# Attention with bias on one core: first loads in float32 in order of need, a first group of three pairs, single banks on VectorE, a ring of 56 banks

## The chip, the cores and the metric

The kernel runs on one core of one Trainium2 chip. The core has TensorE (PE, matrix products into PSUM), VectorE (DVE), ScalarE (ACT), GpSimd (POOL) and SyncE (SP), each with its own in-order queue, and 16 DMA engines that serve the queues of SP, ACT and POOL. The metric is the device time of one execution in microseconds (us); less is better. Before the change the median of three runs is 277.88 us (274.79 to 279.21).

## What is computed

Four batches of eight heads, 1024 positions, head size 64, all float32 in and out:

```python
scores = scale * np.matmul(q, k.transpose(0, 1, 3, 2))      # scale = 1/8
scores = scores + bias                                       # one bias of 1024 x 1024 for all heads
scores_max = np.max(scores, axis=-1, keepdims=True)
attn = np.exp(scores - scores_max) / (np.sum(np.exp(scores - scores_max), axis=-1, keepdims=True) + 1e-8)
return np.matmul(attn, v).astype(np.float32)
```

## The kernel before

**Tiling.** The 32 heads are 16 *pairs*. Rows of q, k, v, bias and the output are dealt out so that partition p holds rows 8p to 8p+7; *chunk* c (0 to 7) is row 8p+c of every p, and "bias row c" below is the slice of bias for chunk c of the queries (128 x 1024 float32, 0.52 MB). The query chunks are handled in three *phases*: A is chunks 6 and 7, B is 3 to 5, C is 0 to 2. The pairs go in three *groups*: pairs 0 and 1 (phases A, B, C), 2 to 7 (C, B, A), 8 to 15 (A, B, C). Within a phase the pairs of the group follow one another, and within a pair its two heads. One head in one phase is two *steps*, one into each of the PSUM buffers sx and sy (three banks of 128 x 512 float32 each): 192 steps in all, 0 to 191. A step of phase A fills two banks, one of B or C three; 512 banks in all.

**A step.** PE computes scores transposed, keys on partitions (`s_fill`, L182). At the first step of a phase, if the phase before was another one, bias is put into PSUM by matmuls with an identity (L169). After that PSUM is never cleared: each fill adds the new head's product and takes the old head's away, with 128 contraction rows of which 64 are the new head and 64 the negated old one. This is why there are two copies of the transposed k and q: KA and QA hold the two heads of a pair (one of q negated), KB and QB hold the first head of the pair beside the second head of the pair before. ACT then takes exp of the buffer and writes bfloat16 into the ring E (`s_exp`, L195), 44 banks long (`EB`). PE multiplies blocks of E with V into `po` (`av_blocks`, L257; V has a column of ones, which gives the row sums), and VectorE divides and stores (`evac`, L267 to L269). No maximum is taken off.

**VectorE's share of exp.** For some pairs of steps the last bank of each is not done by ACT but by VectorE: it is brought into fixed point (`d_fixed`, L207), and six operations (`d_steps`, L219 to L224) on both banks together, 1024 columns, make exp by a polynomial. The result stands in `e` tiles (three buffers) and not in E. 40 of 512 banks go this way.

**Operands.** Each pair's k, q and v are loaded by POOL's queue with a cast to bfloat16 on the way (`load_qk`, `load_v`; three buffers for k and q each, two for v). PE transposes k and q (L137, into `px`), VectorE moves them from PSUM to KA (`k_out`, L140) and QA (`q_out`, L147), makes the negated q (`qn`, L151), and four DMAs on SP's queue copy the halves into KB and QB (L142, L144, L152, L154). KA to QB and V hold nine pairs (`RP`).

**The start** is written by hand (L273 to L324, without the planner): five float32 loads on SP and ACT (k and chunks 6 and 7 of q of pair 0, bias rows 6 and 7) with casts on VectorE and ACT; everything else casting on POOL's queue, in the order k 1, q 1, rest of q 0, v 0, bias rows 3 to 5, v 1, bias rows 0 to 2, k 2, q 2. Seven dummy matmuls keep PE busy until the first data.

**The order of the rest** is made by a planner in the kernel's own Python (`pe_fill`, `pe_piece`, `pe_av`, `pe_pick`, `act_pick`, `dve_pick`) at build time. It keeps a clock for each engine, gives each operation an assumed cost, and at each turn emits the one that can start first; each engine's queue is then fixed. Its numbers are assumptions: `raw_at`, `v_at`, `bias_at` are landing times of the first loads, `DMAL` (2600 ns) is the time from issue to landing of a copy into KB or QB, 1350 ns is the spacing of loads, `RING` (12 steps) says when products with V are overdue, `URG` (6 steps) when a transpose is urgent, `DLIM` how much work VectorE may have queued before it takes banks.

Of the kernel before, what the change touches and what calls it, by code (L numbers as in the profile page):

```python
# [16 lines left out]
def kernel(  # L17
# [11 lines left out]
    nc = tc.nc  # L29
# [14 lines left out]
    EB = 44  # L44
# [6 lines left out]
    de = ctx.enter_context(tc.tile_pool(name="de", bufs=3))  # L51
# [15 lines left out]
    scr = consts.tile([P, 4608], F32)  # L67
    ys = [scr[:, 1024 * i:1024 * (i + 1)] for i in range(2)]
    sf, sb, sp = scr[:, 2048:3072], scr[:, 3072:4096], scr[:, 4096:4608].bitcast(I16)
    c6f, c7f, k0f = scr[:, :1024], scr[:, 1024:2048], scr[:, 2048:3072]  # L70
    q0f = scr[:, 3072:3328]
# [5 lines left out]
    groups = [(range(0, 2), "ABC"), (range(2, 8), "CBA"), (range(8, NP), "ABC")]  # L77
# [61 lines left out]
    def k_out(pr, px):  # L139
        nc.vector.tensor_copy(KA[:, pr % RP, :], px.rearrange("p c q -> p (c q)"))  # L140
        if pr > 1:
            nc.sync.dma_start(out=KB[:D, pr % RP, :], in_=KA[:D, pr % RP, :])  # L142
        if pr + 1 < NP:
            nc.sync.dma_start(out=KB[D:, (pr + 1) % RP, :], in_=KA[D:, pr % RP, :])  # L144

    def q_out(pr, px):
        nc.vector.tensor_scalar(QA[:, pr % RP, :], px.rearrange("p c q -> p (c q)"), sgn[:, :1], None, op0=ALU.mult)  # L147

    def q_neg(pr, c0=0):
        qn = qnp.tile([P, NCH * P], BF, name="qn")  # L150
        nc.vector.tensor_scalar(qn[:], QA[:, pr % RP, :], -1.0, None, op0=ALU.mult)  # L151
        nc.sync.dma_start(out=QB[:D, pr % RP, c0:], in_=qn[:D, c0:])  # L152
        if pr + 1 < NP:
            nc.sync.dma_start(out=QB[D:, (pr + 1) % RP, :], in_=qn[D:, :])  # L154

# [49 lines left out]
    def d_fixed(ch, j, s, b):  # L205
        y = ys[ch % 2].bitcast(I32)
        i = nc.vector.tensor_scalar(y[:, j * 512:(j + 1) * 512], XY[s % 2][:, b * 512:(b + 1) * 512],  # L207
                                    scale * LOG2E * 65536.0, 127.0 * 65536.0, op0=ALU.mult, op1=ALU.add)
        read_of(s, i)

    def d_steps(ch):
        y = ys[ch % 2]
        e = de.tile([P, 1024], BF, name="e")
        dtiles[ch] = e
        lo = y.bitcast(U16).rearrange("p (q w) -> p q w", w=2)[:, :, 0]
        hi = y.bitcast(I16).rearrange("p (q w) -> p q w", w=2)[:, :, 1]
        v_ = nc.vector
        return [
            (690, lambda: v_.tensor_scalar(sf, lo, G / 65536.0, None, op0=ALU.mult)),  # L219
            (690, lambda: v_.tensor_scalar(sp, hi, 0.0, 128.0, op0=ALU.max, op1=ALU.mult)),  # L220
            (1217, lambda: v_.scalar_tensor_tensor(y, sf, U1, sf, op0=ALU.add, op1=ALU.mult)),  # L221
            (1217, lambda: v_.scalar_tensor_tensor(sb, sf, U2, sf, op0=ALU.add, op1=ALU.mult)),  # L222
            (1217, lambda: v_.scalar_tensor_tensor(sb, sb, V2, sp.bitcast(BF), op0=ALU.add, op1=ALU.mult)),  # L223
            (1217, lambda: v_.scalar_tensor_tensor(e[:], y, V1, sb, op0=ALU.add, op1=ALU.mult)),  # L224
        ]
# [11 lines left out]
    def e_block(s, col):  # L237
        b = col // 512
        if (s, b) in d_of:
            ch, j = d_of[s, b]  # L240
            return dtiles[ch][:, j * 512 + col % 512:j * 512 + col % 512 + P]
        return E[:, e_pos[s] * 512 + col:e_pos[s] * 512 + col + P]
# [28 lines left out]
    with tc.manual_schedule():  # L271

        nc.sync.dma_start(out=k0f[:, :NCH * D], in_=kf[0][:, 0])  # L273
        nc.scalar.dma_start(out=c6f, in_=bf_[:, 6, :])
        nc.sync.dma_start(out=q0f.rearrange("p (t x) -> p t x", t=2), in_=qf[0][:, :, 6 * D:])
        nc.sync.dma_start(out=k0f[:, NCH * D:], in_=kf[0][:, 1])
        nc.scalar.dma_start(out=c7f, in_=bf_[:, 7, :])
# [6 lines left out]
        kr0 = raw.tile([P, 2, NCH, D], BF, name="kr")  # L284
        qr0 = raw.tile([P, 2, NCH, D], BF, name="qr")
        load_qk(1)
        nc.gpsimd.dma_start(out=qr0[:, :, :6, :].rearrange("p t c d -> p t (c d)"), in_=qf[0][:, :, :6 * D])
        load_v(0)
        nc.gpsimd.dma_start(out=btraw[:, 3:6, :], in_=bf_[:, 3:6, :])
        load_v(1)  # L290
        nc.gpsimd.dma_start(out=btraw[:, :3, :], in_=bf_[:, :3, :])
        load_qk(2)
        nc.vector.tensor_scalar(ident8[:], ident[:], 1.0 / scale, None, op0=ALU.mult)
# [5 lines left out]
        for i in range(7):  # L299
            dummy(4)  # L300
        nc.vector.tensor_copy(qr0[:, :, 6:, :], q0f.rearrange("p (t c d) -> p t c d", t=2, c=2))
        nc.scalar.copy(kr0[:, 0, :, :], k0f[:, :NCH * D].rearrange("p (c d) -> p c d", d=D))
        pq = ps.tile([P, 2, P], BF, tag="xa", name="px")
        transpose_pe(pq, qr0, 6, 2)
        pk = ps.tile([P, NCH, P], BF, tag="xb", name="px")
        for c in range(NCH):
            nc.tensor.transpose(pk[:D, c, :], kr0[:, 0, c, :], ident[:])
        nc.vector.tensor_scalar(QA[:, 0, 6 * P:], pq.rearrange("p c q -> p (c q)"), sgn[:, :1], None, op0=ALU.mult)
        nc.scalar.copy(QB[:D, 0, 6 * P:], pq[:D].rearrange("p c q -> p (c q)"))
        nc.vector.tensor_copy(btraw[:, 6, :], c6f)  # L310
        nc.scalar.copy(KA[:D, 0, :4 * P], pk[:D, :4].rearrange("p c q -> p (c q)"))
        nc.vector.tensor_copy(KA[:D, 0, 4 * P:], pk[:D, 4:].rearrange("p c q -> p (c q)"))
        s_fill(0)
        s_exp(0, 2, 0)
        nc.vector.tensor_copy(kr0[:, 1, :, :], k0f[:, NCH * D:].rearrange("p (c d) -> p c d", d=D))
        for c in range(NCH):
            nc.tensor.transpose(pk[D:, c, :], kr0[:, 1, c, :], ident[:])
        nc.vector.tensor_copy(btraw[:, 7, :], c7f)
        nc.vector.tensor_copy(KA[D:, 0, :], pk[D:].rearrange("p c q -> p (c q)"))
        s_fill(1)  # L320
        nc.vector.tensor_scalar(QB[D:, 1, 6 * P:], QA[D:, 0, 6 * P:], -1.0, None, op0=ALU.mult)
        nc.vector.tensor_copy(KB[D:, 1, :], KA[D:, 0, :])
        nc.vector.memset(VV[:, :, :, D:], 1.0)
        s_exp(1, 2, 2)  # L324
# [3 lines left out]
        T0 = 8500.0  # L328
        t_act, t_pe, t_dve = T0 + 1830, T0 + 1100, T0 + 1500
        fill_end = [T0, T0 + 900]  # L330
        act_end = [T0 + 915, T0 + 1830]
        fix_end = {}
        x_free = {"xa": T0, "xb": T0 + 1000}
        bias_at = {"A": T0, "B": 15400, "C": 20600}
        raw_at = {(0, 0): 10800, (1, 1): 8500, (1, 0): 9800, (2, 1): 22000, (2, 0): 23300}
        v_at = {0: 11200, 1: 16700}
        dma_t = 23500.0
        kA = {0: T0}
        qA = {(0, "A"): T0}
        kB, qB = {}, {(0, "A"): T0}  # L340
        kB[1] = (T0 + 1900,)
        qB[1, "A"] = (T0 + 1500,)
        pieces = [(1, 1, 0, 4), (1, 1, 4, 4), (1, 0, 0, 4), (1, 0, 4, 4), (0, 0, 0, 6)]
        for pr in range(2, NP):
            pieces += [(pr, w, 0, NCH) for w in (1, 0)]
        cur, cur_tag = [], [None]
        v_ready = {}
        v_todo = [0, 1]
        next_load = 3
        next_v = 2  # L350
        dve_q = []
        mark = {}
        open_ch = {}
        nch = 0
        av_u = 0
        av_items = {}
        av_tag = {}
        av_left = {}
        e_at = {}
        d_at = {}  # L360
        d_load = 0.0
        ch_wait = []
        e_live = [(0, 0, 2), (1, 2, 2)]

        def banks_act(s):
            pa = steps[s // 2][0]
            nb = nbanks(pa)
            return nb - 1 if s in mark else nb
# [8 lines left out]
        def av_make(u):  # L377
            pa, pr, i0 = units[u]
            items = []
            for s in range(2 * i0, 2 * i0 + 4):  # L380
                for b in range(nbanks(pa)):
                    items.append((s, b))
            av_items[u] = items
            for s in range(2 * i0, 2 * i0 + 4):
                av_left[s] = banks_act(s)

        for u in range(NU):
            av_make(u)
# [9 lines left out]
        def operands(s):  # L398
            pa, pr, h, restart = steps[s // 2]
            pk_ = "A" if pa == "A" else "F"  # L400
            if restart:
                if pr not in kA or (pr, pk_) not in qB and (pr, "F") not in qB:
                    return None
                t = qB.get((pr, pk_), qB.get((pr, "F")))
                return max(kA[pr], max(t) if isinstance(t, tuple) else t, bias_at[pa])
            if h:
                t = qA.get((pr, pk_), qA.get((pr, "F")))
                if pr not in kA or t is None:
                    return None
                return max(kA[pr], t)  # L410
            t = qB.get((pr, pk_), qB.get((pr, "F")))
            if pr not in kB or t is None or len(kB[pr]) < 2 or len(t) < 2:
                return None
            return max(max(kB[pr]), max(t))

        def pe_fill():
# [8 lines left out]
            def emit(t):  # L425
                nonlocal nch, d_load
                pa, pr, h, restart = steps[s // 2]
                if h == 0 and s % 2 == 0:
# [356 lines left out]
```

## Time and profile before

| what | value |
|---|---|
| median of three runs | 277.88 us (274.79 to 279.21) |
| the profiled execution: its own time / its span | 276.14 us / 274.0 us |
| mean granted TensorE clock in it | 0.956 |
| busy: PE / DVE / ACT / POOL | 235.8 / 212.9 / 223.9 / 35.5 us |
| exp on ACT (L195) | 96 of three banks, 88 of two, 8 of one |
| L257 products with V, 128 x 65 | 2048, 88.2 us |
| VectorE's exp chain (L207, L219 to L224) | 20 of two banks, 152.5 us |
| loads with a cast (POOL's queue) | 13.83 MB as bfloat16 |
| copies into KB / QB, issue to landing | median 4.6 / 5.1 us, longest 7.3 / 7.4 |

The profile is of one execution; durations are of single instructions, and instructions of one engine overlap by a little, so that their sum is above the engine's busy time. A line of the page's groups reads: source line, engine, operation, result and operand, shapes and count; busy us and mean ns of one; idle time before, and what ended it.

### The profile page before, as it was taken

Reading aid. Unit: us, or ns where it says so; the run is one execution under the profiler, and the core shown is the slowest. Engines: PE = TensorE matmul, PEld = TensorE weight load, DVE = VectorE, ACT = ScalarE, POOL = GpSimd, SP = SyncE. Lnnn points to the kernel's source line nnn. Section 1 sums busy time; section 2 is a strip of 40 time slices with the busy share of each in tenths; the row PEclk is TensorE's granted clock in tenths of the full one; section 3 lists DMA queues with packets and bytes.
Section 4 is the critical chain, followed back from the end, with each engine's and each line's share of the span. In section 5 each row is a group of like instructions: output and inputs, shape, how many; then the busy total and the mean of one; then the engine's idle time right before and its main releaser. Section 6 shows DMA issues by size and latency. Waiting matters only on the chain.

```text
span 274.0 us, 9158 instructions
## 1 busy us (share of the span) xinstructions
PE 235.8 (86%) x3999; PEld 194.7 (71%) x3999; DVE 212.9 (78%) x337; ACT 223.9 (82%) x197; POOL 35.5 (13%) x55
## 2 busy tenths in 40 slices
PE   4889998876899999899895985689998989899983
PEld 1777875654687887699794864577886767778673
DVE  0566988864798999899898586527899998998962
ACT  3277999874798999989997664547999999999993
POOL 8151235233300102100242000000000000000000
PEclk9599999997999999999999799759999999999999
DMA  7999999999961245812999762000221110111112
GB/s 235 221 208 231 206 182 208 211 248 230 178 159 31 44 124 135 156 45 85 139 198 196 159 136 60 19 22 19 60 71 31 60 31 29 32 60 31 60 37 80
DMA packets 31575, 31.94 MB, mean 117 GB/s; under 512 B 2544, under 2 KB 27184, under 8 KB 31536
## 3 DMA queue, kind: packets, MB, share of 16 engines
q0 software_dynamic: 13072, 13.83, 33.1%
q1 hardware_dynamic: 18176, 16.49, 20.5%
q10 hardware_dynamic: 288, 1.05, 1.1%
q8 instruction: 31, 0.51, 0.8%
q14 instruction: 8, 0.07, 0.1%
HBM read 29.36 MB, written 8.39 MB: 138 GB/s over the span
## 4 chain that ended last, share of the span: by engine, by line
PE 44%; ACT 27%; DMA 10%; issue 9%; DVE 7%; POOL 1%; ACTq 1%; SPq 0%; POOLq 0%; DVEq 0%
ACT E L195 27%; PE po L257 13%; PE sx L182 12%; PE sy L182 11%; DMA QB<-qn 5%; PE px L137 3%; DMA scr<-in_q_dram 2%; PE sx L169 2%; DMA vs<-in_v_dram 2%; PE sy L169 2%; DMA KB<-KA 1%; DVE scr L207 1%; DVE ob L268 1%; DVE e L224 1%; DVE KA L140 1%
## 5 line engine op out<-in xcount | busy, mean ns | idle before, releaser
L195 ACT ACTIVATE E<-sx 128x1024 bf16<-128x1024 f32 (+2 forms) x96 | 118.0, 1229 | 23.3 <-PE sx L182 18.7
L195 ACT ACTIVATE E<-sy 128x1024 bf16<-128x1024 f32 (+2 forms) x96 | 117.9, 1228 | 16.1 <-PE po L257 9.3
L257 PE MATMUL po<-VV,E 128*128 128x65 bf16 x1888 | 79.1, 195 | 0.4 <-ACT E L195 0.4
L257 PEld LDWEIGHTS <-E 128*128 128x128 bf16 x1888 | 73.1, 99 | 5.3 <-ACT E L195 0.5
L182 PEld LDWEIGHTS <-KA 128*128 128x128 bf16 (+1 forms) x732 | 55.5, 100 | 23.5 <-issue 11.0
L182 PEld LDWEIGHTS <-KB 128*128 128x128 bf16 x548 | 42.4, 100 | 28.0 <-issue 18.8
L182 PE MATMUL sx<-QB,KB 128*128 128x128 bf16 (+2 forms) x274 | 31.7, 257 | 11.6 <-ACT E L195 4.4
L182 PE MATMUL sy<-QA,KA 128*128 128x128 bf16 (+1 forms) x320 | 36.8, 255 | 5.2 <-ACT E L195 3.9
L182 PE MATMUL sx<-QA,KA 128*128 128x128 bf16 (+1 forms) x320 | 37.1, 257 | 3.7 <-ACT E L195 2.9
L182 PE MATMUL sy<-QB,KB 128*128 128x128 bf16 (+2 forms) x274 | 31.7, 256 | 6.0 <-ACT E L195 5.8
L268 DVE TENSOR_TENSOR ob<-po,rs 128x384 f32<-128x384 f32 (+1 forms) x48 | 24.6, 513 | 1.6
L267 DVE RECIPROCAL rs<-po 128x6 f32<-128x6 f32 (+1 forms) x48 | 9.0, 188 | 20.2 <-PE po L257 20.2
L221 DVE SCALAR_TENSOR_TENSOR scr<-scr 128x1024 f32<-128x1024 f32 x20 | 24.4, 1221 | 0.3
L223 DVE SCALAR_TENSOR_TENSOR scr<-scr 128x1024 f32<-128x1024 f32 x20 | 24.4, 1220 | 0.3
L224 DVE SCALAR_TENSOR_TENSOR e<-scr 128x1024 bf16<-128x1024 f32 x20 | 24.4, 1219 | 0.2
L222 DVE SCALAR_TENSOR_TENSOR scr<-scr 128x1024 f32<-128x1024 f32 x20 | 24.3, 1216 | 0.0
L207 DVE TENSOR_SCALAR scr<-sx 128x512 int32<-128x512 f32 x20 | 13.8, 688 | 9.0 <-PE sx L182 8.8
L128 POOL DMA_DIRECT2D vs<-in_v_dram x16 | 11.5, 716 | 55.7 <-DVE VV L132 44.0
L207 DVE TENSOR_SCALAR scr<-sy 128x512 int32<-128x512 f32 x20 | 13.8, 689 | 4.6 <-ACT E L195 2.5
L122 POOL DMA_DIRECT2D kr<-in_k_dram x15 | 10.9, 727 | 30.2 <-PE px L137 30.1
L169 PEld LDWEIGHTS <-btraw 128*128 128x128 bf16 x152 | 11.8, 151 | 3.6 <-issue 3.1
L140 DVE COPY KA<-px 128x1024 bf16<-128x1024 bf16 x15 | 10.3, 685 | 5.2 <-PE px L137 5.2
(57 smaller groups left out, 162.5 us busy)
## 6 DMA issues: line engine op xcount, KB each, us to landing
out_dram<-ob SPq DMA_DIRECT2D x32, 192.0 KB, 2.0
vs<-in_v_dram POOLq DMA_DIRECT2D x16, 256.0 KB, 5.6
kr<-in_k_dram POOLq DMA_DIRECT2D x15, 256.0 KB, 7.4
qr<-in_q_dram POOLq DMA_DIRECT2D x15, 256.0 KB, 7.4
KB<-KA SPq DMA_DIRECT2D x28, 128.0 KB, 4.6
QB<-qn SPq DMA_DIRECT2D x28, 128.0 KB, 5.1
out_dram<-ob SPq DMA_DIRECT2D x16, 128.0 KB, 2.3
btraw<-in_bias_dram POOLq DMA_DIRECT2D x2, 768.0 KB, 14.1
```

The lines of the kernel that those rows point to most:

```text
L128: nc.gpsimd.dma_start(out=vs.rearrange("p (t c) d -> p t (c d)", t=2), in_=vf[pr])
L140: nc.vector.tensor_copy(KA[:, pr % RP, :], px.rearrange("p c q -> p (c q)"))
L169: nc.tensor.matmul(ps_[:, cc:cc + P], btraw[:, c + j, :].rearrange("p (kp kc) -> p kc kp", kc=NCH)[:, kc, :], ident8[:], start=cc // 512 n ...
L182: nc.tensor.matmul(o, lhsT, rhs, start=False, stop=True, skip_group_check=True)
L195: i = nc.scalar.activation(E[:, pos * 512:(pos + n) * 512], XY[s % 2][:, :n * 512], ACTF.Exp, scale=scale)
L207: i = nc.vector.tensor_scalar(y[:, j * 512:(j + 1) * 512], XY[s % 2][:, b * 512:(b + 1) * 512], scale * LOG2E * 65536.0, 127.0 * 65536.0, ...
L221: (1217, lambda: v_.scalar_tensor_tensor(y, sf, U1, sf, op0=ALU.add, op1=ALU.mult)),
L222: (1217, lambda: v_.scalar_tensor_tensor(sb, sf, U2, sf, op0=ALU.add, op1=ALU.mult)),
L223: (1217, lambda: v_.scalar_tensor_tensor(sb, sb, V2, sp.bitcast(BF), op0=ALU.add, op1=ALU.mult)),
L224: (1217, lambda: v_.scalar_tensor_tensor(e[:], y, V1, sb, op0=ALU.add, op1=ALU.mult)),
L257: nc.tensor.matmul(po[u][:, h, c - c0, :], e_block(s, col), VV[:, pr % RP, h * NCH + kc, :], start=first, stop=left[u] == 0, skip_group_ch ...
L268: nc.vector.tensor_tensor(ob[:], acc[:, :, :, :D], rs[:].to_broadcast([P, 2, W, D]), op=ALU.mult)
```

## The change

- **Loads at the start.** Fifteen float32 loads now stand first on SP and one on ACT, in the order in which their data are used, through bias rows 3 to 5, v of pair 0 and q of pairs 1 and 2. They land in E itself, in banks 8 to 55, which exps reach later (`stage`). VectorE casts q of pair 0 and bias rows 6 and 7, ACT both halves of k of pair 0, POOL all the rest (eleven casts). v 1, v 2 and bias rows 0 to 2 are still cast on the way, behind POOL's casts.
- **Groups.** 0 to 2, 3 to 7, 8 to 15. For pairs 1 and 2 KB and QB are written by VectorE and no longer by DMA where possible, and q is transposed in two parts (chunks 6 and 7 first).
- **VectorE** takes single banks (`d_fixed`, `d_steps` on 512 columns, four `e` buffers), with up to three open. By the new order it takes 37 banks.
- **Ring** of 56 banks; products with V are overdue when 28 banks are in use.
- **Planner.** Later landings are assumed: `DMAL` 4500, loads 2000 apart, `URG` 14. Readiness is kept in one table `R`. A transpose of k or q of pair 3 on is one piece of eight chunks, as it was from pair 2 on.
- Dummy matmuls are 6 of 512 columns and 3 of 256; the memset of V's ones comes earlier.

```diff
-    EB = 44
+    EB = 56
-    de = ctx.enter_context(tc.tile_pool(name="de", bufs=3))
+    de = ctx.enter_context(tc.tile_pool(name="de", bufs=4))
+    st_at = [8 * 512]
+    def stage(n):
+        a = st_at[0]
+        st_at[0] += 2 * n
+        assert st_at[0] <= EB * 512
+        return E[:, a:a + 2 * n].bitcast(F32)
-    groups = [(range(0, 2), "ABC"), (range(2, 8), "CBA"), (range(8, NP), "ABC")]
+    groups = [(range(0, 3), "ABC"), (range(3, 8), "CBA"), (range(8, NP), "ABC")]
...
-        e = de.tile([P, 1024], BF, name="e")
+        e = de.tile([P, 512], BF, name="e")
...
+        sp_ = nc.sync
+        nc.scalar.dma_start(out=sk0, in_=kf[0][:, 0])
+        sp_.dma_start(out=two(sq0), in_=qf[0][:, :, 6 * D:])
+        sp_.dma_start(out=sc[6], in_=bf_[:, 6, :])
+        sp_.dma_start(out=sk0b, in_=kf[0][:, 1])
+        sp_.dma_start(out=sc[7], in_=bf_[:, 7, :])
+        for pr in (1, 2):
+            sp_.dma_start(out=two(sk[pr]), in_=kf[pr])
+            sp_.dma_start(out=two(sq[pr]), in_=qf[pr][:, :, 6 * D:])
+        sp_.dma_start(out=two(sqr[0]), in_=qf[0][:, :, :6 * D])
+        for c in (3, 4, 5):
+            sp_.dma_start(out=sc[c], in_=bf_[:, c, :])
+        sp_.dma_start(out=two(sv0), in_=vf[0])
+        for pr in (1, 2):
+            sp_.dma_start(out=two(sqr[pr]), in_=qf[pr][:, :, :6 * D])
...
+        g = nc.gpsimd
+        cast(g, raws[1, 1].rearrange("p t c d -> p (t c d)"), sk[1])
+        cast(g, *q_part(1, 6, 8, sq[1]))
+        cast(g, raws[2, 1].rearrange("p t c d -> p (t c d)"), sk[2])
+        cast(g, *q_part(2, 6, 8, sq[2]))
+        cast(g, *q_part(0, 0, 6, sqr[0]))
+        for c in (3, 4, 5):
+            cast(g, btraw[:, c, :], sc[c])
+        cast(g, VV[:, 0, :, :D], sv0.rearrange("p (c d) -> p c d", d=D))
         load_v(1)
+        cast(g, *q_part(1, 0, 6, sqr[1]))
+        cast(g, *q_part(2, 0, 6, sqr[2]))
+        load_v(2)
         nc.gpsimd.dma_start(out=btraw[:, :3, :], in_=bf_[:, :3, :])
-        load_qk(2)
...
-        DLIM, DMIN, DTAIL, DMAL, RING, PSL, URG = 3500, 8, 10, 2600, 12, 180, 6
+        DMIN, DTAIL, DMAL, RING, PSL, URG, REM = 8, 4, 4500, 28, 180, 14, 4000
+        T0 = 7000.0
...
+        raw_at = {(1, 1, 0): 9400, (1, 0, 6): 9800, (2, 1, 0): 11500, (2, 0, 6): 12000, (0, 0, 0): 13000,
+                  (1, 0, 0): 19500, (2, 0, 0): 20500}
...
-                dma_t = max(dma_t, t + 2500) + 1350
+                dma_t = max(dma_t, t + 2500) + 2000
...
-            late = len(act_end) - 2 * units[av_u][2] >= RING if av_u < NU else False
+            late = e_used() >= RING
+        def e_used():
+            return sum(av_left[s] for s, p0, n0 in e_live)
```

## The prediction

> **What bounds the kernel now.** First the slices of the page: the span of 274.0 us in 40 slices of 6.85 us, busy shares in tenths.
>
> ```profile
> PE   4889998876899999899895985689998989899983
> ...
> DVE  0566988864798999899898586527899998998962
> ACT  3277999874798999989997664547999999999993
> ...
> PEclk9599999997999999999999799759999999999999
> DMA  7999999999961245812999762000221110111112
> ```
>
> ScalarE (ACT), which does the exponentials, is full in most slices and visibly not in three places: slices 0 to 3, 7 to 9 and 22 to 27. To price these I took the 192 exp instructions in order (step 0 to 191) with their start times. Where they stand back to back, three banks of 512 columns start 1.335 us apart (258.63, 259.96, 261.29), two banks 0.915; one bank is 0.49 by extrapolation. Before has 96, 88 and 8 of them: 128.2 + 80.5 + 3.9 = 212.6 us of ACT work. The first exp starts at 10.91 and the last at 267.94, 6.06 before the end. So 267.94 - 10.91 - (212.6 - 1.3) = 45.7 us are lost between exps. By steps: 0 to 8 lose 4.8, 8 to 24 2.3, 24 to 40 8.9, 40 to 48 0.8, 48 to 104 4.8, 104 to 136 20.9, 136 to 191 3.2. TensorE (PE) is the other candidate, summed below: some 205 us, so also below the span. The kernel is bounded by ACT plus three holes.
>
> Second the chain of waits, start and length in us. In hole two and at the start of hole three its longest links are SBUF-to-SBUF copies into QB and KB:
>
> ```profile
> 50.26 6.25 DMA QB<-qn
> ...
> 60.95 3.96 DMA KB<-KA
> ...
> 144.21 6.29 DMA QB<-qn
> ```
>
> Their issue stands too late in the queues: counting the exps between the issue of a pair's QB copy and the matmuls that first read it, before has 2 to 5 (1.8 to 5.8 us of ACT work) for pairs 2 to 7 and 11 to 15, while such a copy takes 5.1 us in the median and 7.4 at most. Third the list of waits (total us, times, longest):
>
> ```profile
> ACT E L195 <- PE sx L182: 18.7, 18, 3.6
> ACT E L195 <- PE po L257: 13.6, 13, 1.9
> ```
>
> The first line is exp waiting for its scores, at the start and behind late copies; the second is exp waiting for a probability-times-V matmul (po). 12.4 of its 13.6 us lie between 104 and 190 us. The timeline there shows why (start, length, idle before it and releaser):
>
> ```profile
> 163.29 1.02 ACT L195 ACTIVATE E<-sy 128x1024 bf16<-128x1024 f32 x1 [1.01 <-PE po L257]
> 164.37 0.61 PE L182 MATMUL sy<-QA,KA 128*128 128x128 bf16 x8 [1.17 <-ACT E L195]
> ...
> 165.47 0.56 PE L257 MATMUL po<-VV,E 128*128 128x65 bf16 x12
> ...
> 166.00 1.02 ACT L195 ACTIVATE E<-sx 128x1024 bf16<-128x1024 f32 x1 [1.69 <-PE po L257]
> ...
> 167.08 0.61 PE L182 MATMUL sx<-QB,KB 128*128 128x128 bf16 x8 [1.04 <-ACT E L195]
> ```
>
> The exp writes into the ring E of 44 banks, and must wait until po matmuls have read the oldest banks; PE in turn waits for that exp before it can refill the score buffer. Counted from the order of the program, 21 exps (steps 39 to 43 and 111 to 132) have the po matmul that frees their ring space queued behind their own scores: the ring is full and the two engines alternate.
>
> Last the windows of the start (length; busy us and instructions of PE, PEld, DVE, ACT, POOL; clock; DMA share; GB/s):
>
> ```profile
> 4.00:6.00 2.00, 0.16 (x1) 0.00 (x0) 0.00 (x0) 0.62 (x1) 2.00 (x4) 1.00 1.05 391
> ...
> 8.00:10.00 2.00, 1.80 (x16) 1.38 (x15) 1.50 (x4) 0.94 (x2) 0.72 (x1) 0.50 1.25 202
> ```
>
> Float32 loads move 391 GB/s while PE idles for data from 4.2 to 7.4 us, and the granted clock is then 0.50.
>
> **The change, part by part.**
>
> *Start.* Data flow from 2.0 us on (0 to 2 moved 16 GB/s) at 311 GB/s (mean of 2 to 8 us) to 391. In the new order the bytes up to bias row 6 are 0.26 + 0.13 + 0.52 = 0.92 MB: landed at 4.4 to 5.0 us, against 5.5 before, and the q slice no longer at 7.0 but before that. Then the cast of the row on VectorE 0.69, bias matmuls 1.07 and scores 1.03 at the 0.50 clock: first exp at 7.5; 6.4 if PE stays at full clock, 8.5 if something lands late. I take 7.6. The first group is now three pairs: 12 exps in phase A (10 of two banks, 2 of one: 10.1 us), then bias rows 3 to 5. Bytes up to row 5: 4.95 MB, landed at 14.7 to 17.9, take 16.7.
>
> *Casts on GpSimd (POOL).* Before has none there. Nearest rows:
>
> ```profile
> L310 DVE CAST btraw<-scr 128x1024 bf16<-128x1024 f32 x1 | 0.7, 685 | 0.0
> ...
> masks.py:199 POOL TENSOR_SCALAR_AFFINE_SELECT ident<-ident 128x128 bf16<-128x128 bf16 x1 | 0.3, 287 | 0.1
> ...
> masks.py:197 POOL MEMSET ident<- 128x128 bf16 x1 | 0.2, 204 | 0.3 <-POOLq L769 0.3
> ```
>
> The 128-column memset is 0.20 and the select 0.29, against 0.09 for one column: 0.9 and 1.5 ns a column, so 1.0 to 1.65 us for 1024 columns (VectorE's own 0.69 is the floor). Casts for 7,424 columns stand in front of V of pair 1: 7.2 to 12 us, begun when k of pair 1 lands (some 8.6). They mostly trail the landings, so only the last one, 1.3, is on the path: row 5 ready at 18.0, bias 0.9 and scores 0.8, phase B (step 12) at 20.0; bounds 19.3 and 22.6. Before step 8, with 7.3 us of work done, started at 23.08; now 10.1 us are done at 20.0. Behind the casts on POOL are the loads of V 1 and 2 and bias rows 0 to 2. Issued by 22 to 26 and in flight some 9 us (2.6 MB at the 407 GB/s of source bytes that the casting queue reached from 8 to 22 us, plus 2), these land at 31 to 35; phase C needs them at 20 + 15.2 (10 exps of three banks, 2 of two) = 35.2. Hidden, barely.
>
> Whether VectorE slows beside a cast no row shows. Beside POOL's other work it doesn't: VV copies take 0.42 to 0.43 throughout. So 0 from below; from above one cast of 1.3 for each of four VectorE steps in front of phase B's scores, 5 us. I take 0, and keep 5 for a rival.
>
> The Trainium skill ("SBUF — State Buffer", Who interferes with whom) speaks against these casts: GpSimd and VectorE share a port pair, and a VectorE copy in a two-port mode, or an operation with two SBUF inputs, waits out a whole GpSimd instruction that reads SBUF. Nothing in before could show it; by that rule the upper end would hold and the sum be 5 us longer.
>
> *SP's queue.* Fifteen loads now stand first on it, one more on ACT's. From the ninth of these on each waits, in SP's order, for the load eight before it; those have landed by then (row 6 at 5 us for the issue of row 3), so nothing is late. The first copy into KB stands behind them, and is needed only for pair 3.
>
> *Lead of the copies.* In the new order 10 to 13 exps (8.7 to 15.2 us; pair 8: 18.4) stand between the QB copy and its reader, above the 7.4 at most. Hole two and the QB links of hole three close: pairs 1 and 2 get their copies on VectorE (0.68 + 0.42 + some 0.8 us of it, in a stretch where it is a third idle).
>
> *Ring.* 56 banks, and po matmuls brought forward at 28 in use: no exp has its freeing matmul queued behind its own scores. What is late next there is PE itself: a phase-A pair costs 4 x 0.45 scores, 32 x 0.031 po and two transposes of 0.5, 3.8 us, against 3.66 of ACT. Eight pairs lose 1 us.
>
> *Single banks on VectorE.* It takes 37 banks, not 40: three more for ACT, 213.9 us of work (99, 85 and 8 exps). Per bank: 0.69 + 2 x 0.42 + 4 x 0.69 with 0.158 fixed and 1.04 ns a column (from the 424 and 557 ns of 256- and 384-column products), less 0.08 overlap each, 3.8 us; 37 of them 141 us against 20 x 7.1 = 142 before. No gain, no loss. Dummy matmuls, the moved memset and the fourth output buffer cost nothing: PE and VectorE wait for loads there.
>
> **Sum.** Phase B at 20.0; exp work from there to the last start 213.9 - 10.1 - 1.3 = 202.5; residual losses at the rate of the quiet stretch, 4.8 in 56 steps, times 180 steps = 15.4; tail 6.1. Span 244.0. The run took 276.14 for a span of 274.0, and the median of the runs is 277.88: (244.0 + 2.1) x 277.88 / 276.14 = 247.7.
>
> **The rivals.** *Casts too slow.* If a cast takes 1.65 or more, or VectorE is held for one, phase B starts 3 to 5 later, the loads of pair 3 and on move by 4, and C waits 2 to 4 for its bias: 248 + 7 to 14 = 255 to 262. For it: no such row. Against: the leads swallow most. *Half the gain.* Copies wait no more, but the transposes in front of them do: between the issue of a load and its transposes stand 8 to 16 us of exps, while loads took 7.4 in the median but 13.7 to 14.2 when issued in the rush of 8 to 22 us. Three us for each of five pairs: 263; up to 270. Against: before had 10 to 12 us for pairs 5 to 7 and waited 0.2. *Slower: the clock.* PE work is 64 x 0.45 + 128 x 0.66 scores, 2048 x 0.031 po, 32 x 0.5 transposes, 12 bias: 205 us at clock 1.00. The profile shows 0.74 to 0.83 over five windows of 10 us. At 0.75 throughout PE needs 273, the time is 289. It decides from 0.79 down (205/0.79 = 260, no gain). Against: the low clock follows PE's idle stretches, and is 1.00 from 190 to 260 us with PE 0.92 busy. *Not what it says:* the assumed landings don't hold, the holes only move: 272 to 283.
>
> The Trainium skill ("TensorE: Matmul & The Clock Gate", Part 1) has the clock halved after an idle window of some 3.4 us and released by work, which would make the denser queue faster, not slower; the 0.50 above after 3.2 idle agrees.
>
> **How the numbers follow.** Forecast 0.66, 248, its own range 240 to 255 (phase B 19.3 to 22.6, losses 9 to 21); slow casts 0.14; half 0.10; no change 0.04; clock 0.06. Range 240 to 262. Two per cent is about what a measurement of this kernel can tell from no change; faster 0.90, same 0.04, slower 0.06.
>
> **What would show it.** First exp near 7.6 and step 12 near 20; POOL casts of 1.0 to 1.65 us; no wait of scores for QB or KB copies; exp waits for po under 3 us; losses from 104 to 136 of 2 to 4. Wrong would be: PE idle before px for kr landings, VectorE operations stretched while POOL casts, or a clock below 0.9 in dense windows.

## The result and the profile after

The changed kernel takes 249.26 us (median of 4 runs, 248.96 to 249.60), the kernel before beside it 278.54 us (4 runs, 274.79 to 281.31). The ratio is 0.902, with a 95% interval of 0.893 to 0.911. Some executions of a kernel take longer than others of the same kernel, at a lower granted clock, and the ratios here and below leave these out. The profiled run has a span of 247.2 us, 26.8 less than before.

The slices of the changed kernel, now of 6.18 us each:

```profile
DVE  3599998899999899999998979989999999999992
ACT  3688998999999999999998989889999999999992
...
PEclk9999999999999999999999999999999999999999
```

The three places where ScalarE sat below 8 tenths have gone but for the start (its first two slices), and with them every dip of the granted clock. VectorE is 89% busy, TensorE 92%, ScalarE 91%: three engines that can hardly be told apart. The chain of waits (start and length in us) keeps one copy between tiles, where before had the three that the prediction shows:

```profile
140.16 3.06 DMA QB<-qn
```

In the list of waits exp has no entry for a po matmul any more, and its waits for scores are short (total us, times, longest):

```profile
ACT E L185 <- PE sx L172: 5.5, 11, 1.1
ACT E L185 <- PE sy L172: 4.8, 13, 0.7
```

The same count of exps as in the prediction gives: ScalarE's work 213.9, first exp at 8.44, last at 241.09, so 20.1 us lost instead of 45.7. By stretches of steps:

```
steps          before   after
0 to 12          5.5      3.5
12 to 24         1.6      1.9
24 to 42         9.1      1.4
42 to 56         1.7      0.9
56 to 104        3.7      4.1
104 to 136      20.8      5.2
136 to 191       3.3      3.2
```

Of the span's 26.8 us, 7.7 come from steps 24 to 42, 15.6 from 104 to 136, 2.0 from the losses at the start and 2.5 from the earlier first exp; 1.3 us of added exp work count against it. Two more views answer to those of before: the window at the start (length; PE, PEld, DVE, ACT, POOL busy; clock; DMA share; GB/s) and one row of GpSimd's casts, which before had none of.

```profile
8.00:10.00 2.00, 2.00 (x30) 1.73 (x28) 1.66 (x3) 1.02 (x1) 0.50 (x1) 1.00 1.06 383
```

```profile
L265 POOL CAST btraw<-E 128x1024 bf16<-128x1024 f32 x3 | 3.2, 1081 | 1.7 <-DMA E<-in_bias_dram 1.7
```

The clock is 1.00 where it was 0.50 before, and a cast of 1024 columns takes 1.04 to 1.13 us.

### The profile page after: what moved, and what is told of

Read it like the earlier page. It is cut to its first block, busy times and chain, and to the rows that moved or that the text cites. A ratio compares the mean times of both kernels' runs of the same rounds, so it can differ in the third digit from the quotient of the medians.

```text
span 247.2 us, 9283 instructions
## 1 busy us (share of the span) xinstructions
PE 228.5 (92%) x4001; PEld 189.6 (77%) x4001; DVE 220.1 (89%) x443; ACT 225.2 (91%) x198; POOL 40.4 (16%) x59
## 4 chain that ended last, share of the span: by engine, by line
PE 50%; ACT 22%; DVE 13%; issue 10%; DMA 3%; ACTq 1%; DVEq 0%
ACT E L185 22%; PE po L245 14%; PE sx L172 13%; PE sy L172 13%; PE px L144 4%; DVE scr L196 2%; PE sy L159 2%; PE sx L159 2%; DVE scr L210 2%; DMA E<-in_q_dram 1%; DVE QA L556 1%; DMA QB<-qn 1%; DVE ob L256 1%; DVE scr L211 1%; DVE scr L212 1%
## 5 line engine op out<-in xcount | busy, mean ns | idle before, releaser
L185 ACT ACTIVATE E<-sx 128x1536 bf16<-128x1536 f32 (+2 forms) x96 | 117.4, 1223 | 7.5 <-PE sx L172 5.5
L185 ACT ACTIVATE E<-sy 128x1536 bf16<-128x1536 f32 (+2 forms) x96 | 118.7, 1237 | 6.0 <-PE sy L172 4.8
L245 PE MATMUL po<-VV,E 128*128 128x65 bf16 x1900 | 82.8, 194 | 0.7 <-ACT E L185 0.4
L245 PEld LDWEIGHTS <-E 128*128 128x128 bf16 x1900 | 75.2, 98 | 7.4 <-issue 1.0
L210 DVE SCALAR_TENSOR_TENSOR scr<-scr 128x512 f32<-128x512 f32 x37 | 26.0, 702 | 0.8
L212 DVE SCALAR_TENSOR_TENSOR scr<-scr 128x512 f32<-128x512 f32 x37 | 25.5, 690 | 1.0
L213 DVE SCALAR_TENSOR_TENSOR e<-scr 128x512 bf16<-128x512 f32 x37 | 25.5, 690 | 1.0
L211 DVE SCALAR_TENSOR_TENSOR scr<-scr 128x512 f32<-128x512 f32 x37 | 25.3, 683 | 0.0
L209 DVE TENSOR_SCALAR scr<-scr 128x512 int16<-128x512 int16 x37 | 16.2, 437 | 0.0
L135 POOL DMA_DIRECT2D vs<-in_v_dram x15 | 10.9, 727 | 31.8 <-DVE VV L139 29.4
L208 DVE TENSOR_SCALAR scr<-scr 128x512 f32<-128x512 uint16 x37 | 15.7, 425 | 0.0
L196 DVE TENSOR_SCALAR scr<-sx 128x512 int32<-128x512 f32 x20 | 13.7, 686 | 1.7 <-PE sx L172 1.2
L556 DVE TENSOR_SCALAR QA<-px,sgn 128x1024 bf16<-128x1024 bf16 (+2 forms) x18 | 12.2, 679 | 1.5 <-PE px L144 1.4
L196 DVE TENSOR_SCALAR scr<-sy 128x512 int32<-128x512 f32 x17 | 11.7, 688 | 1.9 <-PE sy L172 1.6
```

Source lines behind the costliest of these rows:

```text
L185: i = nc.scalar.activation(E[:, pos * 512:(pos + n) * 512], XY[s % 2][:, :n * 512], ACTF.Exp, scale=scale)
L196: i = nc.vector.tensor_scalar(ys[ch % 2].bitcast(I32), XY[s % 2][:, b * 512:(b + 1) * 512], scale * LOG2E * 65536.0, 127.0 * 65536.0, op0= ...
L208: (360, lambda: v_.tensor_scalar(sf, lo, G / 65536.0, None, op0=ALU.mult)),
L209: (360, lambda: v_.tensor_scalar(sp, hi, 0.0, 128.0, op0=ALU.max, op1=ALU.mult)),
L210: (640, lambda: v_.scalar_tensor_tensor(y, sf, U1, sf, op0=ALU.add, op1=ALU.mult)),
L211: (640, lambda: v_.scalar_tensor_tensor(sb, sf, U2, sf, op0=ALU.add, op1=ALU.mult)),
```

## The experiments

Losses below are counted as above, from each run's own profile. "Lead" is again the ScalarE work between the issue of a QB copy and its reader.

**Undoing one part of the change at a time.** First the urgency of the transposes:

```
-        ... URG, REM = ... 14, 4000
+        ... URG, REM = ... 6, 4000
```

> The kernel after, with one constant set back: a pair's transposes become urgent 6 steps before their pair's first step, as before the change, not 14. In the order of the instructions QB's copies of pairs 3 to 7 and 11 to 15 are then issued 3.2 to 5.5 us of exp work ahead of the scores that read them, where the kernel after has 8.7 or more; a copy of QB took 6.0 us (median) from issue to landing in the kernel after. My theory (the early issue closes the second hole): each of these pairs loses its landing time less its lead less one exp in hand, about 6 us in all, so 253 to 260 us, with idle ScalarE that QB's copies end at steps 28 to 40 and in the last group. Rival 1 (the group of three pairs closed the hole, since its pairs need their copies later): 248 to 251 us, no wait for QB. Rival 2 (the longer landing that the planner assumes closed it): 248 to 251 us as well.

Measured 257.12 us (256.25 to 258.64, ratio to before 0.932 [0.923, 0.941]): 7.9 us above the kernel after, my theory. 5.3 of them are lost in steps 24 to 56. The timeline shows the idle time before exp that the scores end (steps 36 and 44):

```profile
57.13 1.45 ACT L185 ACTIVATE E<-sx 128x1536 bf16<-128x1536 f32 x1 [1.61 <-PE sx L172]
...
69.90 1.45 ACT L185 ACTIVATE E<-sx 128x1536 bf16<-128x1536 f32 x1 [1.32 <-PE sx L172]
```

In the list of waits these scores wait for QB's copies 4 times, 3.9 us in all, 2.0 at the longest, all before 75 us; the kernel after has no such entry. In the last group, where I had expected such waits too, none comes: there 1.2 us more than in the kernel after are lost in steps 104 to 136, with scores that stand behind po matmuls. Groups of three pairs and longer assumed landings are both still in this kernel, so neither replaces the early issue.

> The kernel after with all three assumptions of lead set back together: urgent at 6 steps, copies assumed to land after 2.6 us and not 4.5, loads 1.35 us apart and not 2.0. QB's copies are issued 1.8 to 7.8 us of exp work ahead of their reader. My theory: the same loss as with the urgency alone and some more, 255 to 264 us. Rival (the assumed landing and spacing do the work, urgency little): over 5 us slower than the run with urgency alone set back. Rival (neither, the group of three did it): 248 to 251 us.

Measured 264.27 us (264.04 to 264.56, ratio 0.957 [0.949, 0.965]): 15.0 above the kernel after, just past the upper end of my range, and 7.2 above the run with urgency alone. By its own words that is the rival: assumed landing and spacing have a part of their own. The next run separates them from the urgency. In it the landing assumed for copies changes nothing (with 14 steps of urgency the program comes out the same instruction for instruction for 2,600 and 4,500), so that it tests the spacing of the loads alone, in three places (k, q and v):

```
-                dma_t = max(dma_t, t + 2500) + 2000
+                dma_t = max(dma_t, t + 2500) + 1350
```

> The kernel after with the assumed landings set back (copies 2.6 us, loads 1.35 us apart) but the urgency kept at 14 steps; QB's lead stays at 9.2 us or more in the order of instructions. With urgency set back as well the time was 264.3 us, with urgency alone set back 257.1 us. My theory (the assumed landing matters only where the planner, left to choose, issues a copy as late as it thinks it may; with 14 steps it does not come to that): 248.5 to 250.5 us. Rival (the later landings are worth the 7 us that lie between those two runs, whatever the urgency): 254 to 258 us.

Measured 257.02 us (256.65 to 257.44, ratio 0.933 [0.927, 0.938]). My theory fell, and the rival's 7 us are there: 7.8, whatever the urgency. Most of it lies in one place, steps 36 to 42, which lose 7.4 us where the kernel after loses 0.5. The chain of waits there (pieces that touch end to start):

```profile
51.83 10.90 DMA vs<-in_v_dram
...
62.75 0.43 DVE VV L139
63.18 0.59 DVE scr L212
63.78 0.61 DVE KA L550
...
64.44 1.06 PE px L144 x16
65.50 1.39 PE sy L172 x6
```

Read it forwards. VectorE stands still for 4.86 us before the copy of V into VV, because that pair's load takes 10.9 us to land. Behind this copy in VectorE's order is a copy into KA, which empties a transpose buffer; TensorE waits 4.3 us for that buffer with transposes that stand in front of scores; exp waits 5.5 us for the scores. V itself was not urgent: it is pair 7's, whose first product stands some 20 exps later in the order. The planner put the copy there because it took the load for landed. In the slice from 64 to 70 us the granted clock is down to 5 tenths, and the six score matmuls behind the stall take 1.46 us, where six alike took 0.82 ahead of it.

With that I read the kernel before again. The first link of hole two in its chain, ahead of the QB copy that the prediction showed, is of the same kind, though VectorE stood still only 0.9 us for it:

```profile
40.28 5.51 DMA vs<-in_v_dram
...
45.81 0.43 DVE VV L132
```

**The ring:**

```
-            if pos + n > EB:
+            if pos + n > 44:
```

> The kernel after, with the ring of E wrapped at 44 banks and not 56; all else as after, single banks on VectorE and QB's copies early. In the order of instructions 16 exps (steps 28 to 42 and 114) stand behind a use of E that is issued after their own scores, none in the kernel after. My theory (the ring's size closes the third hole): each blocked exp waits about 0.5 us, so 254 to 260 us, with idle ScalarE ended by TensorE's po matmul in steps 28 to 42. Rival (the late copies alone made the third hole, and the ring was full only because of them): 248 to 251 us, since the copies are early here.

The ratio to before is 0.965 [0.952, 0.978], which is 266.5 us on the 276.28 beside it (median of its runs 269.75): 17 us more than the kernel after, well above my range, with the waits where I had put them. In the profile (span 271.2 us) 26.0 of the 43.9 us lost lie in steps 24 to 42, where the kernel after loses 1.4; but the granted clock is 0.50 to 0.60 there from 54 to 88 us, so I read sizes only from the part ahead of that. The timeline:

```profile
50.54 1.45 ACT L185 ACTIVATE E<-sx 128x1536 bf16<-128x1536 f32 x1 [1.21 <-PE po L245]
...
52.04 0.81 PE L172 MATMUL sx<-QB,KB 128*128 128x384 bf16 x6 [1.35 <-ACT E L185]
...
52.69 0.53 PE L245 MATMUL po<-VV,E 128*128 128x65 bf16 x12
...
53.07 1.45 ACT L185 ACTIVATE E<-sy 128x1536 bf16<-128x1536 f32 x1 [1.09 <-PE po L245]
```

TensorE waits for exp to free a score buffer, then does scores, then the po matmuls that free the ring, and exp waits for these: 2.6 us a step instead of 1.34. A blocked exp costs 1.1 to 1.3 us at full clock, not 0.5. Steps 104 to 136, where before had its large hole, lose 3.6 us here, no more than in the kernel after (5.2): in this kernel a ring of 44 fills up at another place.

**The groups:**

```
-    groups = [(range(0, 3), "ABC"), (range(3, 8), "CBA"), (range(8, NP), "ABC")]
+    groups = [(range(0, 2), "ABC"), (range(2, 8), "CBA"), (range(8, NP), "ABC")]
```

> The kernel after with the groups of before, pairs 0 and 1 first and then 2 to 7, all else as after. QB's copies keep 8.7 us or more of lead. My theory (the group of three gives the start time only, by moving the first need of the bias rows 3 to 5 from the eighth to the twelfth step): the bias rows 3 to 5 land at about 16 us and their casts take 1.04 us each, so the start loses 2 to 5 us: 251 to 255 us, nothing after step 40. Rival (the group of three closes hole 2): 256 us or more, with idle ScalarE in steps 24 to 56. Rival (it is worth nothing): 248 to 250 us.

Measured 253.64 us (253.24 to 253.72, ratio 0.919 [0.909, 0.928]), 4.4 more, my theory. Steps 0 to 24 lose 8.9 us (after: 5.4), 24 to 56 lose 2.9 (after: 2.3). The chain shows the cause, bias row 5 needed before it is cast; exp waits 2.04 us for the scores behind it. Another 1.0 us comes behind the last exp (7.1 us to the end, 6.1 in the kernel after).

```profile
8.19 9.61 DMA E<-in_bias_dram
17.86 1.05 POOL btraw L265
```

**One part alone, on the kernel before.** Here the ring is tried at 52 banks, not 56: twelve more banks take 12 KB of each partition, and 9 of them come, in the change, from the scratch that single banks on VectorE halve (18 KB to 9). That 56 don't fit without it no run shows.

```
-        ... DMAL, RING, PSL, URG = ... 2600, 12, 180, 6
+        ... DMAL, RING, PSL, URG = ... 4500, 12, 180, 14
-                ... + 1350          (three places)
+                ... + 2000
```

> The kernel before with the planner's lead alone: urgent at 14 steps, copies assumed to land after 4.5 us, loads 2.0 us apart. In the order of instructions QB's copies are then issued 7 to 12 us of exp work ahead of their reader, but with the ring of 44 banks 14 exps (steps 30 to 41, 111 to 115, 123, 124) stand behind a use of E issued after their own scores. My theory, after the run with the ring set back: lead without room in E turns the wait for QB into a wait for po, so 270 to 285 us, with idle ScalarE ended by po at steps 30 to 41. Rival (the lead closes both holes by itself): 258 to 266 us.

```
-    EB = 44
+    EB = 52
```

> The kernel before with a ring of 52 banks and not 44, nothing else; QB's copies still have 2.7 to 5.3 us of lead, one exp (step 131) is blocked and not 21. My theory (the ring made most of the third hole, the late copies the second): the second hole of about 9 us stays, the third falls from 21 to about 8 us: 263 to 271 us. Rival (the third hole came from late copies, the full ring was its consequence): 273 to 282 us.

> The kernel before with both: the lead (14 steps, 4.5 us, 2.0 us) and a ring of 52 banks; one blocked exp, 7 us of lead or more. Loads, groups and pairs of banks on VectorE are those of before. My theory: second and third hole both close, the late start (6.3 us later at the twelfth step) stays: 278 less 7 and less 16 is 255, so 252 to 260 us, and the run with the kernel after's groups undone (253.6 us) is about the same. Rival (single banks on VectorE are needed too): over 262 us.

```
kernel                       us    ratio to before, 95%    lost 24-42  104-136
before (beside these)      276.31                              9.1      20.8
lead alone                 262.66   0.953 [0.945, 0.962]       3.3      12.5
ring of 52 alone           265.55   0.958 [0.946, 0.971]       6.9       8.3
lead and ring of 52        253.15   0.919 [0.913, 0.926]       0.7       3.9
```

With the lead alone my theory fell: 262.66 us, in the rival's range. The rival's reason holds for hole two alone, since the third hole still loses 12.5. Hole two nearly closes although 7 of its exps are blocked in the order of the instructions: two of them wait for po, 2.6 us in all, and for the others the po matmuls come in time. A count of blocked exps is therefore no price, and why a ring of 44 costs so much more in these steps of the kernel after stays open. The ring alone did as I expected: its scores still wait 7.1 us for QB copies, and the third hole is down to 8.3. The two together give 23.2 us, close to the sum of 13.7 and 10.8, and within 4 us of the whole change with the old loads, old groups and pairs of banks: rival refuted, single banks on VectorE aren't needed for themselves.

It is also the time of the kernel after with the old groups (253.64 us). With those, the float32 loads, the single banks, the last four banks of the ring and the rest of the change together bring nothing: the first exp starts 2.6 us earlier (8.64 against 11.28), and 0.8 us more of exp work, 0.4 more of losses and 1.1 more behind the last exp use that up. No run sets the float32 loads back alone.

Then the groups of three on top of that kernel:

> The kernel before with lead and a ring of 52 banks (253.15 us) and also the groups of the kernel after, pairs 0 to 2 first; loads still in bf16 through GpSimd's queue, pairs of banks on VectorE. It has no blocked exp. My theory (the group of three pays only because the float32 loads bring pair 2 and the bias rows in time; here pair 2 comes after the bias through one queue): 253 to 259 us. Rival (the group of three gives the 4.4 us that it was worth in the kernel after whatever the loads are): 248 to 250 us.

Measured 263.70 us (263.49 to 265.15, ratio 0.958 [0.953, 0.964]): 10.6 slower than without them. Both ranges fell. Steps 4 to 8 lose 12.8 us, 12.0 of them in one wait, and the chain ends it with a QB copy of 7.65 us that is issued only at 27.74, after transposes of Q that waited for a buffer which po matmuls of the first pairs held. I had blamed the loads; the chain names the buffer and the copy. In the kernel after pair 2's first copies are made on VectorE, 0.22 to 0.97 us each, and no such link exists. What is worth 4.4 us there costs 10.6 here.

**VectorE's banks in phase A.** In the kernel after, an exp of one bank ends early, but the next starts 0.94 us after it:

```profile
147.54 0.63 ACT L185 ACTIVATE E<-sx 128x512 bf16<-128x512 f32 x1
148.48 1.02 ACT L185 ACTIVATE E<-sy 128x1024 bf16<-128x1024 f32 x1 [0.31 <-PE sy L172]
```

```
-                if s >= DMIN and s < NS - DTAIL and s - 1 not in mark ...
+                if pa != "A" and s >= DMIN and s < NS - DTAIL and s - 1 not in mark ...
```

> The kernel after, but VectorE takes no banks in the phase of two blocks per step; 31 of its banks in all and not 37, ScalarE's work 216.4 us and not 213.9. My theory (a single-bank exp there ends early, but the next exp starts 0.92 us after it all the same, so that the bank saves no time): 247.5 to 250.5 us. Rival (each of those banks saves ScalarE its 0.43 us): 251 to 253 us.

Measured 249.38 us (248.66 to 250.06), the time of the kernel after. ScalarE has 2.5 us more work and loses 1.8 less (18.3), and VectorE's share falls from 89 to 79%. The eight banks that VectorE takes in phase A (two of them move to other phases here) buy next to nothing there.

**GpSimd's casts beside VectorE.** After each `load_qk`, on two scratch tiles of its own:

```
+        for i in range(8):
+            nc.gpsimd.tensor_copy(xd[:], xs[:])
```

> The kernel after with GpSimd made to cast a scratch tile of 128x256 from float32 to bf16 eight times after each of its 13 pairs of K and Q loads, some 40 us of casts beside a VectorE that is 89% busy. This prices what the prediction took at nothing, VectorE's operations held beside GpSimd's casts (at the start five operations were 0.2 to 0.7 us longer beside casts of 128x1024, 2.5 us in all). Theory of the hold: VectorE's operations beside these casts take up to 0.5 us longer, VectorE loses 10 to 30 us, and the time is 254 to 275 us. Rival (a held operation is short, the rest is slack): 248.5 to 251 us.

Measured 256.45 us (254.67 to 257.81, ratio 0.931 [0.924, 0.937]): 7.2 more, within the theory of the hold; its upper part, 10 us and more for VectorE, did not come. VectorE's busy time rises from 220.1 to 226.7 us. Between 40 and 140 us (busy us, mean ns of one), first the extra casts' run, then the kernel after, the same operation:

```profile
L213 DVE TENSOR_SCALAR scr<-scr 128x512 int16<-128x512 int16 x14 | 7.3, 519 | 0.0
```

```profile
L209 DVE TENSOR_SCALAR scr<-scr 128x512 int16<-128x512 int16 x15 | 6.3, 421 | 0.0
```

The four products of the chain, which read two operands in SBUF, rise from 683 to 690 ns to 728 to 752. What reads its data from PSUM does not rise: the copies into KA 688 and 679, the first step of a bank 687 and 682. The casts themselves take 526 ns here in the mean and 400 at the least. The loads behind the casts on GpSimd's queue are also later (VectorE waits 3.7 us for V loads, 0.3 in the kernel after), so how much of the 7.2 us is the hold alone stays open.

The Trainium skill ("SBUF — State Buffer", Who interferes with whom) has this split: VectorE and GpSimd share one port pair, an operation with two SBUF inputs or in a two-port mode is kept out by a GpSimd instruction that reads SBUF, and one that needs neither is not. The rows agree for the products and for what reads PSUM; the row that rises most has one input in SBUF, and in which mode it runs no row shows.

**An earlier step 4.** In the planner's table:

```
-        raw_at = {(1, 1, 0): 9400, (1, 0, 6): 9800, ...
+        raw_at = {(1, 1, 0): 9000, (1, 0, 6): 9200, ...
```

> The kernel after with the planner told that pair 1's K and Q are cast 0.4 and 0.6 us earlier (in its own clock, which runs about 1.4 us ahead of the chip), so that K's transposes of pair 1 are queued on TensorE ahead of the scores of step 3 and not behind them. In the kernel after TensorE stood idle 0.56 us before those scores with the cast K at hand from 10.54 us, and the exp of step 4 came 1.08 us late. My theory: step 4's exp starts at 13.1 to 13.6 us and not 14.15, and the time falls by 0.5 to 1.0 us to 248.2 to 248.8 us. Rival (something later is late by then, so that the start does not carry through): 249.0 to 249.8 us.

Measured 249.76 us (6 runs, 248.75 to 251.08; ratio 0.907 [0.902, 0.912]): no gain, and no version better than the kernel after was found. In the profiled run (span 249.1) the first exp starts at 7.31 but step 4 only at 15.99, because bias row 7 and pair 1's K land 1.2 us later than in the profile of the kernel after, and K's transposes now delay the scores of step 3. Whether the order alone would have gained in a run with the earlier landing I cannot say.

## Why the prediction was right, and where it was not

The forecast was 248.0 and the time is 249.26; 244.0 was the span, 247.2 came.

- *Start, step 12 at 20.0: came at 21.96.* The first exp was at 8.44, not 7.6; losses make the rest. The bound I used, bias row 5 ready at 18.0, was nearly right (its cast ended at 18.56) and was not the limit: it was ScalarE's 10.1 us of work from 8.44 on, plus 3.5 lost, of it 1.2 at step 4 by pair 1's K (landed 9.50, cast 1.04, then transposes behind scores), 0.9 at step 1 by bias row 7 and 0.6 at step 12. (The loads up to row 5 add up to 4.98 MB, not 4.95.) 2.0 of the 3.2 us missing are this term.
- *Casts on GpSimd at 1.3 us:* 1.04 to 1.13, near the floor of my range, and they trail the landings.
- *VectorE beside them took 0:* wrong in kind, small in size. Five operations at the start were longer by 2.5 us in all, the 5 us of the upper end did not come, and the steady rate of the run with extra casts is 6.6 us of VectorE for 54.5 us of casts. None of the five stood on the path to step 4.
- *Lead of the copies closes hole two:* the urgency gives the lead and is worth 7.9 us. But the step is incomplete: it read the QB links in the chain and passed over the V load in front of them. The spacing of the loads, for which the sum has no term, is worth 7.8 us by itself, since it moves VectorE's copy of V behind the landing. Only the last rival had asked whether the assumed landings hold, and nothing in the prediction looks at when the V of pair 3 and on lands: that the sum came out without this is luck.
- *Ring of 56, no blocked exp:* exp's waits for po went from 13.6 us to no entry in the list. The ring of 44 costs 17 us in the new kernel and the ring of 52 gains 10.8 in the old one. Hole three was made by both, ring and late copies, as the runs on the kernel before show; the prediction had named both, not their shares.
- *Single banks, no gain, no loss:* right for the time, not in its parts. Summed over its instructions VectorE's exp chain takes 159.6 us for 37 banks, against 152.5 for 40 in before, where the prediction had 141 against 142; with VectorE 89% busy this had room. And the prediction did not see that the banks in phase A save ScalarE next to nothing. What single banks do give is most of the room for the ring.
- *Residual 15.4:* 16.6 came between step 12 and the end, near the rate I took, with steps 104 to 136 above it at 5.2 against 2 to 4 expected.
- *Rivals.* Slow casts fell on the 1.04 us; the clock fell on a mean of 1.000; the transposes' wait for loads did not come, yet its mechanism is real: loads that land later than planned gave 257 us where the planner was told the old spacing. The holes did not move.

## What to carry to other kernels

Where an order is written out in advance, each assumed landing is a wait planted in an in-order queue: an operation that isn't urgent, put before its data has landed, holds everything behind it, here 7.8 us from one number. So walk the chain of waits back to the first link that isn't an engine, and not to the first that fits. A ring in front of an in-order engine has to hold what that engine has queued ahead, and parts of a change are priced only in the kernel that they stand in: the group of three pairs gained 4.4 us where pair 2's copies are made on VectorE and cost 10.6 where they go by DMA.

## What was not expected of the hardware

- A V load of 256 KB (as bfloat16) issued among others took 10.9 us to land, against 5.1 in the median of the kernel after (4.0 to 14.4 there).
- The granted clock dips behind a long stall that the queues make: 9 tenths in all 40 slices of the kernel after, 5 tenths in the slice from 64 to 70 us of the kernel with the loads' old spacing, where TensorE had stood idle for 4.3 us. That stall was dearer than its length: scores took 1.46 us behind it and 0.82 ahead of it.
- In the run with extra casts, VectorE's steps of exp that work on SBUF are 40 to 100 ns longer in the mean, its bfloat16 copies within SBUF 16 to 20 (423 to 443 and 426 to 442), and what reads PSUM not at all; the casts take 526 ns in the mean and 400 at the least.
